# A hybrid decoder trunk on one core: the mixer's weights are split in two pieces of 512 columns instead of four of 256

## The chip, the core and the metric

The kernel runs on one core of a Trainium2 chip (trn2). The metric is the device time of one execution in microseconds. Before the change the median of three runs is 1102.03 us, from 1096.82 to 1108.56. About 1% (11 us) is what a measurement of this kernel can tell from no change.

## What is computed

Two layers (DEPTH = 2) over 256 tokens of 1024 channels, all in float32:

```python
for l in range(DEPTH):
    x = layer_norm(ALPHA * x + swiglu_half(x, ffn1_w1[l], ffn1_w3[l], ffn1_w2[l]), ln1_g[l], ln1_b[l])
    h = x @ w_in[l]
    (a_u, a_v, b_qkv, b_z, b_beta, b_decay, c_q, c_k, c_v, c_r, c_g) = jnp.split(h, split_at, axis=-1)
    out_a = spatial_gating(...)     # chunked gating MLP
    out_b = gated_deltanet(...)     # short conv, triangular solve in chunks of 64, scan over 4 chunks
    out_c = gla(...)                # gated linear attention, chunks of 64
    x = layer_norm(ALPHA * x + concat([out_a, out_b, out_c]) @ w_out[l], ln2_g[l], ln2_b[l])
    x = layer_norm(ALPHA * x + swiglu_half(x, ffn2_w1[l], ffn2_w3[l], ffn2_w2[l]), ln3_g[l], ln3_b[l])
```

## The kernel before

All weights stand in one array `w_all` of units, each 128 partitions by 1024 float32 columns (eight 128x128 tiles). A layer has 167 units: 66 of the first FFN, 35 of the mixer, 66 of the second FFN. A unit is loaded by one DMA into a raw buffer (five of them, SP's queue), then turned into two tiles of the type fp32r: `wh` is the rounded weight (a cast on ACT, L199), `wl` is what the rounding left out (raw minus `wh`, a subtraction on DVE, L200). The activations are split likewise into xH and xL, and one float32 product is three matmuls (`mm3`, L227 to L229: wh·xH, wh·xL, wl·xH). There are five `wh` and five `wl` buffers. `done` (L212) converts ahead, so that two units lie converted behind the one just finished.

`conv` (L184) cuts a unit's conversion into pieces: one cast and one subtraction each. The number of pieces comes from `CUTS` (L41) by the unit's place i in the mixer: one piece for i < 9 (the seven units misc, m, z, r and the first two k units), four pieces for i from 9 to 34, one in the FFNs. Four mixer units of each layer (`WHOLE`, L55: au0, cv0, cv1, v3) are multiplied raw, with no conversion. So 26 - 4 = 22 units of a layer, 44 in all, are converted in four pieces of 256 columns. A loop over pieces issues cast, subtraction, cast, subtraction; a new load of the raw buffer is asked for after the last piece (L202).

Each engine takes its instructions in one fixed order. The order is made at build time by a scheduler, which places what is ready and goes by priorities and its own costs. `ORDER` (L42) is the order in which the mixer's tasks are handed to it, `PIN` (L43) names tasks that may not come ahead of the end of the solve.

The mixer of a layer runs like this. The units misc, m, z, r; then four k and four q units with a short convolution behind each (L565, three times L567); the squares of q and k are summed on PE (`pss`, L698), ACT takes logarithms (L724), and DVE builds the decay matrices (L726 to L782). `t_sub` (L817 to L836) is a long chain on DVE that inverts 16x16 blocks; its end is L834, called the solve here. PE has filler meanwhile: pcv, pau, pav, pv, and transposes of k (`ptk`, L895). Then `t_l0` and `t_l1` join the blocks with small matmuls (p1a L850, L852 on DVE, p2a L856, p1b L870, p2b L877), with v and z units as filler. Then the scan over four chunks: `t_s` (pX), `t_d` and `t_dk` (the matrix XP, L924, L932; POOL's product qd at L933), `t_c` (S at L1075, u, po), and the output projection `yo`. The unit pau1 needs the PSUM bank that L932 frees.

Of the kernel before, what the change touches and what calls it, by code (L numbers as in the profile page):

```python
# [37 lines left out]
HP0, HP1, HP2, HP7 = 0, 400, 300, 0  # L38
CONST = 3
EVAC = 12  # L40
CUTS = ((9, 1), (17, 4), (35, 4))  # L41
ORDER = "v0 sub cv a0 tk0 zz av v3 v1 l0a l0b z3 l1a v2 zr l1b tk1 avn tv z1 zm s0 cq s1 d1 d0 dk a1 c0 pp kt t0 sc s2 c1 t1 s3 c2 pz w1 po c3 t2 w3 t3 w0 w2".split()  # L42
PIN = set("tk0 av v3 v1 l0a z3 l1b tk1 avn z1 s1 pp t0 s2 c1 c2 w1 po c3 t3 w2".split())  # L43
UNITS = {"a0": ("au", 0), "a1": ("au", 1), "av": ("av", 0), "cv": ("cv", 0), "v0": ("v", 0), "v1": ("v", 1),
# [79 lines left out]
def trunk(ctx: ExitStack, tc: tile.TileContext, xin, w_all, cin, pin, lin, gin, out, dbg=None, nlayers=L):  # L124
# [59 lines left out]
    def conv(upto):  # L184
# [11 lines left out]
        i = b % NU - 3 * NF  # L196
        w = 1024 // next((c for o, c in CUTS if 0 <= i < o), 1)
        for o in range(0, 1024, w):
# [1103 lines left out]
```

## Time and profile before

| what | value |
|---|---|
| median of the runs | 1102.03 us |
| the profiled execution | 1108.28 us, of which the span from first to last instruction is 1106.5 us |
| busy: PE, DVE, ACT, POOL | 1062.1, 753.9, 600.4, 78.6 us |
[...]
| conversions on DVE (L200) and ACT (L199) | 413.8 and 353.2 us, 455 instructions each |

A busy PE is not a PE at full speed: matmuls overlap in the pipeline, and a matmul that was issued while the clock stood at half speed takes about twice as long. In the FFN stretches PE issues a matmul of 256 columns every 0.11 us. The mixers lie at about 189 to 345 us and 736 to 897 us of the span.

### The profile page before, as it was taken

The page shows a single profiled execution, that of the slowest core. Times are in us where ns is not written, and L with a number is a line of the kernel's source. Part 1 is how long each engine was busy: PE and PEld are TensorE (multiplying, and loading weights), DVE is VectorE, ACT ScalarE, POOL GpSimd, SP SyncE. Part 2 cuts the span into 40 slices and gives each one's busy share as a digit, 9 for nine tenths or more (in the row PEclk, how much of TensorE's full clock was granted, in tenths as well). Part 3 has the DMA queues.
Part 4 walks back from the last instruction along what each step waited for, and adds up shares of the span by engine and source line. Part 5 has one row for each costly group of instructions (what it writes and reads, how often), then busy time and mean ns, then how long its engine had stood idle before and what let it go on. Part 6 is the DMA issues. An engine that isn't in the chain of part 4 may idle for free. (4 is left out here: it accounts for less than half of the span.)

```text
span 1106.5 us, 23698 instructions
## 1 busy us (share of the span) xinstructions
PE 1062.1 (96%) x9875; PEld 1012.5 (92%) x9875; DVE 753.9 (68%) x1262; ACT 600.4 (54%) x1063; POOL 78.6 (7%) x62
## 2 busy tenths in 40 slices
PE   8999999999999899999989999999989998999996
PEld 7999999987889899999889999999787897999995
DVE  4555556989867965555786555579896679655556
ACT  5444445777556744444664444468664567444442
POOL 0100001101002200000220000020000012000000
PEclk9999999999999999999989999999996999999999
DMA  8855554442323375555336656534331234655541
GB/s 275 303 194 193 193 198 161 153 135 77 116 78 123 138 244 191 192 195 198 140 118 225 193 195 198 195 136 162 124 114 62 97 115 154 229 195 191 191 165 39
DMA packets 51515, 182.38 MB, mean 165 GB/s; under 512 B 5840, under 2 KB 7376, under 8 KB 51280
## 3 DMA queue, kind: packets, MB, share of 16 engines
q1 hardware_dynamic: 50544, 177.23, 47.6%
q10 hardware_dynamic: 864, 3.64, 0.9%
q8 instruction: 77, 1.26, 0.4%
q14 instruction: 30, 0.25, 0.1%
HBM read 179.81 MB, written 1.05 MB: 163 GB/s over the span
## 5 line engine op out<-in xcount | busy, mean ns | idle before, releaser
L200 DVE TENSOR_TENSOR wl<-raw,wh 128x1024 fp32r<-128x1024 f32 (+1 forms) x455 | 413.8, 926 | 236.9 <-ACT wh L199 236.6
L199 ACT CAST wh<-raw 128x1024 fp32r<-128x1024 f32 (+1 forms) x455 | 353.2, 800 | 365.8 <-issue 183.1
L227 PE MATMUL h<-x,wh 128*128 128x256 f32 x864 | 238.7, 276 | 0.0
L228 PE MATMUL h<-x,wh 128*128 128x256 f32 x864 | 238.6, 276 | 0.0
L229 PE MATMUL h<-x,wl 128*128 128x256 f32 x864 | 238.6, 276 | 0.0
L228 PEld LDWEIGHTS h<-x,wh 128*128 128x128 f32 x864 | 162.2, 188 | 0.8
L227 PEld LDWEIGHTS h<-x,wh 128*128 128x128 f32 x864 | 162.2, 188 | 0.7
L229 PEld LDWEIGHTS h<-x,wl 128*128 128x128 f32 x864 | 162.2, 188 | 0.0
L227 PE MATMUL y<-gs,wh 128*128 128x256 f32 x528 | 147.0, 279 | 7.2 <-ACT gs L232 7.2
L228 PE MATMUL y<-gs,wh 128*128 128x256 f32 x528 | 147.2, 279 | 0.0
L229 PE MATMUL y<-gs,wl 128*128 128x256 f32 x528 | 147.1, 279 | 0.0
L228 PE MATMUL h<-xL,wh 128*128 128x256 f32 (+1 forms) x472 | 132.9, 282 | 2.3 <-DVE xL L342 2.1
L227 PE MATMUL h<-xH,wh 128*128 128x256 f32 (+1 forms) x472 | 134.0, 284 | 0.8 <-ACT wh L199 0.7
L229 PE MATMUL h<-xH,wl 128*128 128x256 f32 (+1 forms) x472 | 133.2, 282 | 0.5 <-DVE wl L200 0.5
L227 PEld LDWEIGHTS y<-gs,wh 128*128 128x128 f32 x528 | 100.1, 190 | 7.6 <-ACT gs L232 7.6
L228 PEld LDWEIGHTS y<-gs,wh 128*128 128x128 f32 x528 | 100.6, 191 | 0.0
L229 PEld LDWEIGHTS y<-gs,wl 128*128 128x128 f32 x528 | 100.5, 190 | 0.0
L228 PEld LDWEIGHTS h<-xL,wh 128*128 128x128 f32 x472 | 90.5, 192 | 3.2 <-DVE xL L342 2.9
L227 PEld LDWEIGHTS h<-xH,wh 128*128 128x128 f32 x472 | 90.6, 192 | 1.7 <-ACT wh L199 1.2
L229 PEld LDWEIGHTS h<-xH,wl 128*128 128x128 f32 x472 | 90.5, 192 | 1.0 <-DVE wl L200 0.9
L430 DVE TENSOR_TENSOR g<-s,h 128x256 f32<-128x256 f32 x76 | 32.0, 421 | 45.8 <-PE h L229 37.3
L345 POOL TENSOR_TENSOR s<-x 128x512 f32<-128x512 f32 x5 | 7.1, 1416 | 520.7 <-DVE x L338 520.7
(363 smaller groups left out, 1960.9 us busy)
## 6 DMA issues: line engine op xcount, KB each, us to landing
raw<-w_all SPq DMA_DIRECT2D x331, 512.0 KB, 3.7
raw<-w_all SPq DMA_DIRECT2D x12, 128.0 KB, 4.1
pl<-pin ACTq DMA_DIRECT2D x2, 730.5 KB, 7.2
cst<-cin ACTq DMA_DIRECT2D x1, 1026.0 KB, 8.6
x<-xin SPq DMA_DIRECT2D x4, 256.0 KB, 4.2
out<-xT SPq DMA_DIRECT2D x4, 256.0 KB, 2.0
Gb<-gin ACTq DMA_DIRECT2D x1, 512.0 KB, 3.5
Bb<-gin ACTq DMA_DIRECT2D x1, 512.0 KB, 4.0
```

Of the source, the lines that this page charges most:

```text
L199: st["copy"] = A.copy(WH[b][:, o:o + w], raw[b][:, o:o + w])
L200: V.tensor_sub(WL[b][:, o:o + w], raw[b][:, o:o + w], WH[b][:, o:o + w].bitcast(F32))
L227: PE.matmul(o, lhsT=wh, rhs=mh, start=first, stop=False, **kw)
L228: PE.matmul(o, lhsT=wh, rhs=ml, start=False, stop=False, **kw)
L229: PE.matmul(o, lhsT=wl, rhs=mh, start=False, stop=last, **kw)
L345: G.tensor_tensor(s2, x[:, 0:2], xs, op=ALU.add)
L430: V.tensor_mul(g, s, h3[:, :T])
```

## The change

```diff
-CUTS = ((9, 1), (17, 4), (35, 4))
+CUTS = ((9, 1), (35, 2))
```

`conv` reads the table: the 44 units are cut in two pieces of 512 columns instead of four of 256. ACT has 88 casts fewer and DVE 88 subtractions fewer; the columns converted, the loads and the matmuls are the same. The orders of POOL and SP are the same, word for word; PE has the same matmuls in a slightly different order. The scheduler moved other work too, in both layers alike; three places follow, those of layer 0.

PE at the end of the k and q units, where `pss` is the last of the four sums of squares (pcv is a unit multiplied raw, pv a v unit). Before:

```order
L227 MATMUL pv_3075<-xH,wh_2882 128x256
L228 MATMUL pv_3075<-xL,wh_2882 128x256
L229 MATMUL pv_3075<-xH,wl_2883 128x256
L631 MATMUL pcv<-raw_2715,x 128x256 x2
L698 MATMUL pss<-sqkq,cst 32x512
L631 MATMUL pcv<-raw_2715,x 128x256 x2
L631 MATMUL pcv<-raw_2758,x 128x256 x4
```

After:

```order
L227 MATMUL pv_3043<-xH,wh_2858 128x256
L228 MATMUL pv_3043<-xL,wh_2858 128x256
L229 MATMUL pv_3043<-xH,wl_2859 128x256
L631 MATMUL pcv<-raw_2703,x 128x256
L698 MATMUL pss<-sqkq,cst 32x512
L631 MATMUL pcv<-raw_2703,x 128x256 x3
L631 MATMUL pcv<-raw_2742,x 128x256 x2
```

The last `pss` stands behind one matmul of pcv instead of two. Further on, 16 transposes `ptk` stand ahead of p1a instead of 27 (the 11 others come right behind it), and 8 matmuls of the z unit ahead of p2a instead of 13. On DVE, one of four L586 (for the z and m units) moved from behind L726 to ahead of it; between L726 and the solve no piece stands before or after.

DVE right behind the solve (kb, kd: scaled transposes; wl: the pieces; acc: the convolution of a v unit; iv at L852: what p2a waits for). Before:

```order
L904 TENSOR_TENSOR kb<-ptk,es 128x512
L905 TENSOR_TENSOR kd<-ptk,kds 128x512
L200 TENSOR_TENSOR wl_3272<-raw_2930,wh_3271 128x256 x4
L200 TENSOR_TENSOR wl_3284<-raw_2932,wh_3283 128x256 x4
L567 SCALAR_TENSOR_TENSOR acc<-pv_3295,pl,acc 128x255
L200 TENSOR_TENSOR wl_3337<-raw_2944,wh_3336 128x256
L567 SCALAR_TENSOR_TENSOR acc<-pv_3295,pl,acc 128x254
L200 TENSOR_TENSOR wl_3337<-raw_2944,wh_3336 128x256
L567 SCALAR_TENSOR_TENSOR acc<-pv_3295,pl,acc 128x253
L200 TENSOR_TENSOR wl_3337<-raw_2944,wh_3336 128x256 x2
L567 SCALAR_TENSOR_TENSOR acc<-pv_3311,pl,acc 128x255
L852 TENSOR_TENSOR iv_3062<-p1a,cst 128x256
```

After:

```order
L904 TENSOR_TENSOR kb<-ptk,es 128x512
L905 TENSOR_TENSOR kd<-ptk,kds 128x512
L200 TENSOR_TENSOR wl_3236<-raw_2902,wh_3235 128x512 x2
L200 TENSOR_TENSOR wl_3244<-raw_2904,wh_3243 128x512 x2
L567 SCALAR_TENSOR_TENSOR acc<-pv_3251,pl,acc 128x255
L200 TENSOR_TENSOR wl_3293<-raw_2912,wh_3292 128x512
L567 SCALAR_TENSOR_TENSOR acc<-pv_3251,pl,acc 128x254
L200 TENSOR_TENSOR wl_3293<-raw_2912,wh_3292 128x512
L567 SCALAR_TENSOR_TENSOR acc<-pv_3251,pl,acc 128x253
L567 SCALAR_TENSOR_TENSOR acc<-pv_3267,pl,acc 128x255
L852 TENSOR_TENSOR iv_3030<-p1a,cst 128x256
```

Six pieces instead of twelve stand ahead of the first L852.

DVE ahead of L932 (which frees the bank for pau) and of L1075 (the first state S of the scan). Before:

```order
L971 COPY_PREDICATED PTs<-cst,pPT 128x512 x2
L200 TENSOR_TENSOR wl_4138<-raw_3346,wh_4137 128x256
L932 TENSOR_TENSOR XP<-pkq,XP 128x512
L200 TENSOR_TENSOR wl_4138<-raw_3346,wh_4137 128x256
L932 TENSOR_TENSOR XP<-pkq,XP 128x512
L200 TENSOR_TENSOR wl_4138<-raw_3346,wh_4137 128x256 x2
L200 TENSOR_TENSOR wl_4242<-raw_3529,wh_4241 128x256 x4
L200 TENSOR_TENSOR wl_4290<-raw_3605,wh_4289 128x256
L1075 COPY S<-pS 128x256
```

After:

```order
L971 COPY_PREDICATED PTs<-cst,pPT 128x512 x2
L200 TENSOR_TENSOR wl_4074<-raw_3298,wh_4073 128x512
L200 TENSOR_TENSOR wl_4174<-raw_3477,wh_4173 128x512
L932 TENSOR_TENSOR XP<-pkq,XP 128x512 x2
L200 TENSOR_TENSOR wl_4174<-raw_3477,wh_4173 128x512
L200 TENSOR_TENSOR wl_4218<-raw_3549,wh_4217 128x512
L1075 COPY S<-pS 128x256
```

Two pieces of 512 stand between L971 and the first L932 instead of one of 256, and the piece right ahead of L1075 has 512 columns instead of 256. That piece's cast on ACT, too, is the first instruction behind ACT's wait for pau in both orders.

## Rows read from the trace of the kernel before

**Rows 1.** The page's first part: busy us, share of the span, instructions.

```profile
PE 1062.1 (96%) x9875; PEld 1012.5 (92%) x9875; DVE 753.9 (68%) x1262; ACT 600.4 (54%) x1063; POOL 78.6 (7%) x62
```

**Rows 2.** Windows, mixer of layer 0: stretch, length, busy us (instructions) of PE, PEld, DVE, ACT, POOL, PEclk, DMA.

```profile
211.00:245.00 34.00, 34.00 (x299) 29.41 (x297) 31.41 (x84) 27.21 (x70) 0.00 (x0) 1.00 0.43 144
272.90:299.60 26.70, 24.83 (x554) 22.38 (x554) 21.27 (x56) 12.90 (x32) 0.00 (x0) 0.87 0.32 103
```

**Rows 3.** Windows, mixer of layer 1: the stretch from p1a to pX.

```profile
819.70:852.20 32.50, 30.43 (x552) 27.25 (x552) 21.76 (x58) 13.32 (x32) 0.00 (x0) 0.68 0.26 83
```

**Rows 4.** Waits of PE, 185 to 350 us: us in total, times, longest.

```profile
PE p1a L850 <- DVE iv L833: 1.9, 1, 1.9
PE pau L227 <- DVE XP L932: 1.9, 1, 1.9
PE p2a L856 <- issue: 1.7, 1, 1.7
```

**Rows 5.** Waits of PE, 743 to 908 us.

```profile
PE p1a L850 <- DVE iv L833: 2.8, 1, 2.8
PE p1b L870 <- issue: 2.1, 1, 2.1
```

**Rows 6.** Groups of instructions by form: count, busy us, mean ns, idle before.

```profile
L200 DVE TENSOR_TENSOR wl<-raw,wh 128x256 fp32r<-128x256 f32 x176 | 71.8, 446 | 6.9 <-ACT wh L199 6.8
```

**Rows 7.** Timeline, DVE: start us, us from first start to last end, line, form, count.

```profile
209.84 1.89 DVE L384 TENSOR_TENSOR x<-x,rs 128x512 f32<-128x512 f32 x3
...
274.68 2.75 DVE L200 TENSOR_TENSOR wl<-raw,wh 128x256 fp32r<-128x256 f32 x8
```

**Rows 8.** Timeline, ACT: four casts of 256; a cast of 512 and its follower.

```profile
234.68 1.31 ACT L199 CAST wh<-raw 128x256 fp32r<-128x256 f32 x4
...
331.89 0.61 ACT L232 CAST mAC<-mc 128x512 fp32r<-128x512 f32 x1
332.41 0.47 ACT L166 ACTIVATE sqb<-pqb,cst 128x256 f32<-128x256 f32 x1
```

**Rows 9.** Timeline, PE, around the last pss and the transposes behind it.

```profile
243.21 1.02 PE L631 MATMUL pcv<-raw,x 128*128 128x256 f32 x4
244.16 1.04 PE L698 MATMUL pss<-sqkq,cst 128*32 128x512 f32 x2
...
255.96 1.50 PE L895 MATMUL ptk<-cst,KQ 64*64 64x64 f32 x44
```

**Rows 10.** Timeline, ACT: the squares that the last pss reads.

```profile
242.05 0.64 ACT L703 ACTIVATE sqkq<-KQ 128x512 f32<-128x512 f32 x1
```

**Rows 11.** Timeline, DVE, around L726; in brackets: idle before, and its releaser.

```profile
242.88 0.88 DVE L586 SCALAR_TENSOR_TENSOR zrm<-muN,zrm 128x256 f32<-128x256 f32 x2
...
245.74 0.41 DVE L726 SCALAR_TENSOR_TENSOR RT<-lnn,gam 8x256 f32<-8x256 f32 x1 [1.31 <-ACT lnn L166]
```

**Rows 12.** Timeline, DVE, ahead of the first L852: layer 0, then layer 1.

```profile
279.19 0.75 DVE L200 TENSOR_TENSOR wl<-raw,wh 128x256 fp32r<-128x256 f32 x2
280.08 0.48 DVE L567 SCALAR_TENSOR_TENSOR acc<-pv,pl,acc 128x255 f32<-128x255 f32 x1
...
826.65 0.48 DVE L567 SCALAR_TENSOR_TENSOR acc<-pv,pl,acc 128x255 f32<-128x255 f32 x1
827.04 0.42 DVE L852 TENSOR_TENSOR iv<-p1a,cst 128x256 f32<-128x256 f32 x1
```

**Rows 13.** Timeline, DVE, ahead of the first L932.

```profile
305.73 1.95 DVE L200 TENSOR_TENSOR wl<-raw,wh 128x256 fp32r<-128x256 f32 x1
```

**Rows 14.** Timeline, POOL, at the same time.

```profile
305.05 2.35 POOL L933 TENSOR_TENSOR qd<-qd,KQ 128x1024 f32<-128x1024 f32 x1 [1.09 <-ACT qd L166]
```

**Rows 15.** Timeline, ACT and then DVE, behind the unit pau.

```profile
312.88 0.40 ACT L199 CAST wh<-raw 128x256 fp32r<-128x256 f32 x1 [5.57 <-PE pau L228]
...
313.31 0.42 DVE L200 TENSOR_TENSOR wl<-raw,wh 128x256 fp32r<-128x256 f32 x1 [2.08 <-ACT wh L199]
```

**Rows 16.** Waits of PE, 312.9 to 345 us: all there are.

```profile
PE pu L1058 <- DVE S L1077: 0.2, 1, 0.2
```

## The prediction

> **What bounds the kernel now.** First the page's busy times: PE is busy for 1062.1 us of a span of 1106.5 us, DVE for 753.9, ACT for 600.4 [rows 1]. PE does the bulk of the work, so an edit on ACT and DVE can only win time where PE waits for them, or where PE runs below its full clock because it has waited. Next, the windows of the mixer of layer 0. While the k and q units run (211 to 245 us) PE is busy for all 34.00 us at clock 1.00, although DVE is busy for 31.41 of them [rows 2]: there the conversions are hidden. [...] Last the waits of PE: for the solve 1.9 and 2.8 us, for L932 1.9 us, and 1.7 and 2.1 us in the middle of p2a or p1b for which the profile names nobody [rows 4, 5]. All waits of a mixer come to some 6 or 7 us; that is nearly all that there is to win or lose, apart from the clock.
>
> **What the change takes off ACT and DVE.** 176 pieces of 256 columns [rows 6] become 88 of 512. The mean durations there must not be multiplied, since one piece starts before the last has ended. In a run, eight pieces take 2.75 us, 0.344 each; three subtractions or products of 512 columns take 1.89 us, 0.63 each [rows 7]. A unit on DVE goes from 4 x 0.344 = 1.38 to 2 x 0.63 = 1.26 us, 0.12 less. On ACT four casts take 1.31 us in a run; a cast of 512 takes 0.61 us and lets its follower start 0.52 us after itself [rows 8], so two take 0.52 + 0.61 = 1.13, 0.18 less. Over 44 units that is 5.3 us off DVE and 7.9 us off ACT. Half of it belongs to either layer, and most lies beside a PE that doesn't wait. [...]
>
> **The change place by place**, against the profiled execution (1108.28 us, 6.3 above the median of the runs; a difference found in it is taken off the median as it is). Bounds are for both layers together.
>
> *The k and q units: 0.* The second pair of xL now stands behind two pieces of 512 instead of two of 256, 2 x (0.63 - 0.344) = 0.57 us later, and the first matmuls on it can slip as much. PE now has a third k unit's matmuls to put there. Bounds 0 and +1.1; I take +0.2. That a matmul waits for a whole piece costs nothing while the unit was converted two units ahead, as now; without that cover a unit would wait 0.63 - 0.344 = 0.29 us.
>
> *The solve: -1.0.* The last pss runs at 244.16, though its squares are done at 242.05 + 0.64 = 242.69 [rows 9, 10]: it waits in PE's queue behind two matmuls of pcv, 244.16 - 243.21 = 0.95 us. With one ahead it comes 0.48 us earlier. ACT's logarithms follow, then L726, which now waits 1.31 us [rows 11]; a moved L586 (0.88 / 2 = 0.44 us) fits in that wait and leaves the chain behind it. Together the solve could end 0.48 + 0.44 = 0.92 us earlier in each mixer. But 11 transposes now come behind p1a: 44 rows of them (two rows a transpose) take 1.50 us [rows 9], so 22 rows are 0.75 us that PE has still to do. Where PE sets the pace behind p1a, the gain is 0.17; where the chain does, 0.92. The stretch is mixed [rows 2, 3], so I take the middle, 0.5 a layer. Bounds -1.8 and 0.
>
> *Behind the solve: -0.4.* The first L852 now has six pieces ahead instead of twelve: 6 x 0.63 - 12 x 0.344 = -0.35 us. In layer 0 DVE is done with its pieces at 279.94 and waits until 280.08 for a convolution that PE feeds, so the gain is hidden; in layer 1 it doesn't wait, and L852 follows at once [rows 12]. One layer gains: -0.4 in round numbers; bounds -0.7 and 0.
>
> *Ahead of L932: +0.6.* The piece in front of it took 1.95 us, where another took 0.42 [rows 15], while POOL ran its product for 2.35 us [rows 13, 14], from 305.05 to 307.40: the piece ended 0.28 us behind that. After the change two pieces stand there. If the second falls under the product, it ends later by 0.29 us, what 512 columns cost more than 256; if the first does, the second comes on top, 0.63. PE's pau waits for L932 already [rows 4], so this goes on the path. I take 0.3 a layer; bounds 0 and +1.3.
>
> *Ahead of the first S: +0.6.* ACT stands 5.57 us in a wait for pau, and the first thing behind is a cast; DVE waits 2.08 us for it before its piece, and S comes behind [rows 15]. Cast and piece grow by 0.52 - 0.33 = 0.19 and 0.29 us, 0.48 together. PE's only recorded wait up to the end of the mixer is 0.2 us for an S [rows 16], so some of this is hidden by other small matmuls. I take 0.3 a layer; bounds 0 and +1.0.
>
> Sum: 0.2 - 1.0 - 0.4 + 0.6 + 0.6 = 0.0, between -2.5 and +3.4. From the profiled 1108.3 that stays 1108.3, and from the median 1102.0. POOL and SP keep their orders, so that no load or product is asked for at another place; the FFNs are as they were.
>
> **The rivals.** *The clock comes back.* What ended 5.8 us later in layer 1 than in layer 0 is the same work at a lower clock [rows 2, 3]. Each of these stretches begins behind a wait of PE for the solve [rows 4, 5]. The change moves these waits and the work around them; if layer 1 then runs like layer 0, the time is 1102 - 5.8 = 1096. All of both low-clock parts would give 0.13 x 26.7 + 0.32 x 32.5 = 13.9 us, 1088. For it: it differs already between two layers. Against it: the solve still comes after PE's filler, since p1a's wait stays at 1.9 - 0.92 + 0.75 = 1.7 us.
>
> *The clock goes lower: the other side.* Only 8 matmuls of z stand ahead of p2a, not 13; at 34.00 / 299 = 0.114 us a matmul [rows 2], 5 x 0.114 = 0.6 us of filler is gone where PE needs L852's result. A new wait there would follow that for the solve closely. If layer 0 then runs as layer 1 does, the time is 1102 + 5.8 = 1108; if both lose as much, 1114. It decides as soon as L852 ends behind z's eighth matmul. [...]
>
> *Coarse pieces stall PE.* If the conversions were only just in time, each of the 44 units would wait 0.29 us: 12.8 us, 1115. Against it: 34.00 busy of 34.00 us in the k and q stage [rows 2].
>
> *ACT is worth more than the rows say.* If ACT's queue held up the chain at every unit and saved the 0.18 us of rows 8 and DVE the 0.12 of rows 7 one behind the other, 44 x 0.30 = 13.2 us would go: 1089. Against it: ACT is busy for 12.90 of 26.70 us behind the solve [rows 2]. [...]
>
> **How the numbers follow.** Terms cancel: 0.53. Clock comes back in one layer: 0.17, in both: 0.04. Clock lower in one layer: 0.15, in both: 0.04. Coarse pieces: 0.04. ACT worth more: 0.03. The likeliest is 1102.0 us, alone between 1099.5 and 1105.4 by the bounds. The range takes in one layer's clock either way and the runs' own spread (1096.82 to 1108.56): 1094 to 1110. Both-layer cases and the last two, 0.15, lie outside. Faster by over 1% (under 1091): 0.07; slower by over 1% (over 1113): 0.08; within 1%: 0.85. About 1% is what a measurement of this kernel can tell from no change.
>
> **What would show it.** The groups of instructions should have 88 pieces of 512 columns at some 0.69 us on DVE and 0.61 on ACT; if these are much longer, the sum is wrong. The solve should end 0.9 us earlier counted from the first k matmul, with p1a's wait between 1.5 and 2 us. L852 of layer 1 should come 0.4 us sooner behind kb; PE's wait for L932 should be as long or 0.3 us longer. PE should still not wait in the k and q stage. The windows behind the solve should have mean clocks between 0.68 and 0.87; a clock outside that in both layers would make the prediction wrong, as would a wait of several us of PE for `wh` or `wl`.

## The result, and the profile after

| | before | changed |
|---|---|---|
| median of 20 runs each, us | 1102.42 (1095.63 to 1112.93) | 1095.03 (1088.96 to 1103.85) |
| ratio changed / before, 95% interval | | 0.9935 [0.9905, 0.9964] |
| profiled execution, us (span) | 1108.28 (1106.5) | 1099.81 (1097.9) |

All ratios, and the mean clocks given with them, leave out executions that took over 1.5% longer than the fastest of the same kernel.

The changed kernel is faster by 0.65%, some 7 us. That is within the 1% that was called no change, and inside the range of 1094 to 1110; but the forecast was that the terms cancel, at 1102, and they don't.

First the page's busy times and the groups by form of the changed kernel (columns as in [rows 1] and [rows 6]):

```profile
PE 1057.2 (96%) x9875; PEld 1009.1 (92%) x9875; DVE 744.0 (68%) x1174; ACT 593.2 (54%) x975; POOL 80.0 (7%) x62
```

```profile
L200 DVE TENSOR_TENSOR wl<-raw,wh 128x512 fp32r<-128x512 f32 x88 | 58.6, 689 | 6.7 <-ACT wh L199 6.2
L199 ACT CAST wh<-raw 128x512 fp32r<-128x512 f32 x88 | 51.7, 616 | 21.6 <-PE pz L228 7.1 <-PE pau L228 4.9 <-PE pr L228 2.9
```

The pieces cost what was forecast (0.69 and 0.61 us). DVE and ACT are busy for 10 and 7 us less; that as such is worth nothing, as the experiments show. Now waits of PE in the mixer of layer 0, then of layer 1 (us in total, times, longest), to be held against [rows 4] and [rows 5]:

```profile
PE p1a L850 <- DVE iv L833: 2.3, 1, 2.3
PE pz L229 <- issue: 2.1, 1, 2.1
PE pau L308 <- ACT cv L642: 0.9, 1, 0.9
```

```profile
PE p1a L850 <- DVE iv L833: 2.4, 1, 2.4
PE pmisc L228 <- DVE xL L342: 1.0, 1, 1.0
PE pau L308 <- ACT cv L642: 0.9, 1, 0.9
PE pv L229 <- DVE wl L200: 0.6, 1, 0.6
```

One more of the trace before belongs beside them, in layer 1:

```profile
PE pau L227 <- DVE XP L932: 1.8, 1, 1.8
```

Two things are gone: in both layers PE's wait for L932 (1.9 us in [rows 4], 1.8 in layer 1), and in layer 1 the wait at p1b that the profile gives to "issue", that is, to nobody (2.1 us [rows 5]). In layer 0 such a wait stays (1.7 before, 2.1 now). The windows from p1a to pX, layer 0 and layer 1 of the changed kernel, against the second row of [rows 2] and against [rows 3]:

```profile
278.90:304.40 25.50, 23.36 (x574) 21.18 (x574) 21.51 (x46) 12.20 (x24) 0.00 (x0) 0.93 0.37 121
820.90:845.90 25.00, 24.41 (x574) 22.37 (x574) 21.61 (x46) 12.21 (x24) 0.00 (x0) 0.86 0.37 116
```

Layer 0 goes from 26.70 to 25.50 us, layer 1 from 32.50 to 25.00, at a mean clock of 0.86 in place of 0.68. Where the clock of layer 1 came from shows in a finer cut. Before, PE at work until 831.1, the wait, and what follows:

```profile
825.00:831.10 6.10, 6.09 (x180) 5.51 (x180) 5.95 (x17) 2.89 (x9) 0.00 (x0) 1.00 0.69 214
831.10:833.10 2.00, 0.00 (x0) 0.00 (x0) 1.26 (x4) 0.21 (x1) 0.00 (x0) 1.00 0.00 0
833.10:838.00 4.90, 4.85 (x63) 4.35 (x63) 1.86 (x5) 1.66 (x5) 0.00 (x0) 0.67 0.50 166
834.80:851.90 17.10, 17.10 (x195) 15.14 (x195) 8.20 (x22) 6.52 (x14) 0.00 (x0) 0.50 0.13 44
```

The same work in the changed kernel:

```profile
830.80:834.40 3.60, 3.60 (x163) 3.40 (x164) 3.55 (x9) 0.72 (x2) 0.00 (x0) 1.00 0.04 15
834.40:838.00 3.60, 3.60 (x76) 3.22 (x70) 2.64 (x6) 1.96 (x5) 0.00 (x0) 1.00 0.52 166
838.00:842.00 4.00, 4.00 (x81) 3.47 (x81) 3.80 (x11) 1.99 (x4) 0.00 (x0) 1.00 0.37 121
```

Before, PE ran no instruction at all for 2.0 us, and then ran at half its clock (0.50) for 17.1 us although it was busy all the time; matmuls of 256 columns started 0.215 us apart there (834.58 to 836.30 us, records of 0.41 us each) and 0.115 at 1.00 (829.50 to 830.42 us, records of 0.28). In the changed kernel there is no such gap and the clock stays at 1.00. From the first p2a to the first pX that is 24.3 us before and 15.1 after (827.9 to 852.2, 830.8 to 845.9): the wait of 2.1 us, and 7 us that go with the low clock. The wait for the solve, at the start of these stretches, is in both kernels, and in both the clock is low behind it, in the changed kernel for longer. Layer 1, before and then changed:

```profile
821.10:824.50 3.40, 3.38 (x23) 3.11 (x22) 3.40 (x10) 1.86 (x6) 0.00 (x0) 0.51 0.17 39
```

```profile
822.70:829.50 6.80, 6.21 (x44) 5.88 (x43) 5.26 (x12) 2.22 (x6) 0.00 (x0) 0.50 0.59 181
```

Behind pX, up to the first po, layer 0 goes from 14.2 to 11.2 us, layer 1 from 14.1 to 11.2. The two windows of layer 0, before and after:

```profile
299.60:313.80 14.20, 12.35 (x179) 10.33 (x178) 12.12 (x26) 8.55 (x18) 4.65 (x3) 0.88 0.37 124
```

```profile
304.40:315.60 11.20, 11.20 (x193) 9.28 (x192) 8.59 (x17) 8.69 (x16) 4.89 (x3) 1.00 0.46 153
```

These differences come to 14.6 us (1.2 + 7.5 + 3.0 + 2.9), twice the gain of the medians. The profiled execution of before lies 6 us above its median, and that of the changed kernel lost 7 us in the first FFN, which the change doesn't touch (last section): the trace shows where time went, the medians how much.

### The profile page after: what moved, and what is told of

Same layout as the page of the kernel before. It is cut to its first block, busy times and chain, and to the rows that moved or that the text cites. A ratio compares the mean times of both kernels' runs of the same rounds, so it can differ in the third digit from the quotient of the medians.

```text
span 1097.9 us, 23518 instructions
## 1 busy us (share of the span) xinstructions
PE 1057.2 (96%) x9875; PEld 1009.1 (92%) x9875; DVE 744.0 (68%) x1174; ACT 593.2 (54%) x975; POOL 80.0 (7%) x62
## 3 DMA queue, kind: packets, MB, share of 16 engines
q8 instruction: 77, 1.26, 0.5%
## 4 chain that ended last, share of the span: by engine, by line
PE 77%; DVE 17%; issue 3%; ACT 2%; DMA 1%; DVEq 0%; SPq 0%; ACTq 0%
PE h L229 13%; PE h L228 13%; PE h L227 13%; PE y L227 5%; PE y L228 5%; PE y L229 5%; DVE wl L200 4%; PE y L520 2%; PE y L522 2%; PE y L521 2%; DVE xL L342 2%; PE h L308 1%; DVE acc L567 1%; DVE x L338 1%; PE yo L227 1%
## 5 line engine op out<-in xcount | busy, mean ns | idle before, releaser
L200 DVE TENSOR_TENSOR wl<-raw,wh 128x1024 fp32r<-128x1024 f32 (+1 forms) x367 | 400.0, 1098 | 241.4 <-ACT wh L199 240.5
L199 ACT CAST wh<-raw 128x1024 fp32r<-128x1024 f32 (+1 forms) x367 | 342.8, 946 | 369.1 <-issue 192.1
```

The source lines that it names most:

```text
L199: st["copy"] = A.copy(WH[b][:, o:o + w], raw[b][:, o:o + w])
L200: V.tensor_sub(WL[b][:, o:o + w], raw[b][:, o:o + w], WH[b][:, o:o + w].bitcast(F32))
```

## The experiments

Three explanations of the 7 us stood at first: the place (PE's wait for L932 and what hangs on it), the spread (0.17 us at each of the 44 units), and the front (the solve comes sooner). The first four runs tried these. They turned up a fourth, the instructions, which the other eight runs test; in those, theory P stands for all explanations by the pieces themselves.

All results in one table. "Issue" are PE's waits for nobody, of 0.4 us or more, behind p1a; p2a to pX and pX to po are taken from the first starts of these tiles in the trace, to some 0.1 us; "clock" is the mean granted clock of a kernel's executions (of before beside them: 0.980, 0.982, 0.978 and 0.981 in the four sets of runs: 1 to 4, 5 to 8, 9 to 11, 12).

| kernel | ratio to before, 95% | clock | issue L0 / L1, us | p2a to pX, L0 / L1 | pX to po, L0 / L1 |
|---|---|---|---|---|---|
| before | | | 1.7 / 2.1 | 18.2 / 24.3 | 14.2 / 14.1 |
| changed | 0.9935 [0.9905, 0.9964] | 0.986 | 2.1 / 0 | 17.4 / 15.1 | 11.2 / 11.2 |
| 1: k and q in two | 0.9991 [0.9952, 1.0029] | 0.980 | 1.7 / 1.6 | 16.8 / 23.9 | 14.2 / 10.4 |
| 2: later units in two | 0.9949 [0.9913, 0.9986] | 0.985 | 2.4 / 0 | 17.7 / 15.6 | 11.2 / 11.2 |
| 3: before, pieces held | 0.9986 [0.9945, 1.0028] | 0.978 | 1.6 / 1.7 | 18.2 / 23.9 | 10.3 / 10.3 |
| 4: before, POOL later | 0.9989 [0.9951, 1.0027] | 0.982 | 2.2 / 2.6 | 17.3 / 26.0 | 11.0 / 10.8 |
| 5: before, shift 128 | 0.9964 [0.9928, 1.0000] | 0.983 | 0 / 1.2 and 1.1 | 14.8 / 16.3 | 14.2 / 14.2 |
| 6: before, shift 256 | 1.0008 [0.9966, 1.0049] | 0.983 | 0.8 / 0.8 | 15.9 / 15.8 | 12.7 / 14.2 |
| 7: changed, shift 128 | 0.9904 [0.9865, 0.9944] | 0.985 | 0 / 0 | 15.1 / 15.1 | 11.2 / 11.2 |
| 8: changed, shift 40 | 0.9912 [0.9875, 0.9948] | 0.985 | 0 / 0 | 15.0 / 15.8 | 11.1 / 11.2 |
| 9: before, shift 160 | 0.9913 [0.9877, 0.9949] | 0.985 | 0.8 / 0 | 15.9 / 14.9 | 14.2 / 14.2 |
| 10: pieces held, shift 160 | 0.9872 [0.9824, 0.9920] | 0.987 | 0.7 / 0 | 15.8 / 14.9 | 10.1 / 10.1 |
| 11: changed, shift 64 | 0.9885 [0.9841, 0.9929] | 0.986 | 0 / 0.9 | 15.1 / 16.3 | 11.2 / 11.2 |
| 12: changed, shift 256 | 0.9906 [0.9870, 0.9942] | 0.986 | 2.2 / 0.4 | 17.6 / 15.7 | 11.1 / 11.1 |

### 1 and 2: half of the units each

```
-CUTS = ((9, 1), (17, 4), (35, 4))
+CUTS = ((9, 1), (17, 2), (35, 4))
```

and, for the second,

```
-CUTS = ((9, 1), (17, 4), (35, 4))
+CUTS = ((9, 1), (17, 4), (35, 2))
```

> Only the k and q units and v0 (7 units a layer, 14 in all) are cut in two; all later units stay in four. The change as a whole won 7 us (1102.4 to 1095.0). Theory A, the place: the gain is PE's wait for L932 (1.9 us in layer 0, 1.8 in layer 1) and the low clock behind it, pX to the first po going from 14.2 to 11.2 us; here the pieces ahead of L932 are as before, so PE's wait for L932 stays near 1.9 us and the time within 2 us of before. Theory B, the gain is spread over the 44 units, 7.4 / 44 = 0.17 us each: 14 x 0.17 = 2.4 us faster. Theory C, the front: the solve comes sooner (my own term, -1.0) and brings clock with it: 3 to 6 us faster, p1a to pX shorter in layer 1 than before's 24 to 32 us.

> Only the units behind v0 (15 units a layer, 30 in all) are cut in two; k, q and v0 stay in four. Theory A, the place (PE's wait for L932): no piece stands between L954 and L971 any more, the wait is gone, 6 to 7 us faster than before, as the whole change. Theory B, spread: 30 x 0.17 = 5.1 us faster. Theory C, the front: 0 to 3 us faster.

Measured: 0.9991 and 0.9949. The later units carry the gain; the k and q units, and with them the front, have none that can be told. The gain of the second, 0.51% or 5.6 us, lies between what A and B said, so the time does not part these two. The trace does more: in 1 the wait at p1b is there (1.6 us, layer 1 from p2a to pX 23.9 us), in 2 it is gone (15.6 us), as in the changed kernel. In 2, too, eight matmuls of z stand ahead of p2a, and in 1 thirteen.

### 3: the pieces of w3 and w0 held behind L932

```
-            V.tensor_sub(WL[b][:, o:o + w], raw[b][:, o:o + w], WH[b][:, o:o + w].bitcast(F32))
+            r = V.tensor_sub(WL[b][:, o:o + w], raw[b][:, o:o + w], WH[b][:, o:o + w].bitcast(F32)); 28 <= i < 30 and behind(r, st["dk"])
...
-                V.tensor_tensor(PT[:, cs], pkq[c2], XP[:, cs], op=ALU.mult)
+                st["dk"] = V.tensor_tensor(PT[:, cs], pkq[c2], XP[:, cs], op=ALU.mult)
```

> The kernel before, all pieces still 256 columns; only the pieces of w3 and w0 are held behind the second L932, so that none stands between L954 and L932 (before: seven, one of which took 1.95 us). Theory A, the place: L932 runs 2 to 3 us sooner, PE's pau does not wait for it, 4 to 7 us faster (3.7 us of waits in both layers, more if the clock behind it stays up). Theories B and C: within 1 us of before, since no unit and nothing ahead of the solve is changed.

Measured: 0.9986 [0.9945, 1.0028]. The place is mended as meant. DVE's timeline around L932, in which L932 now waits for PE and not PE for it:

```profile
303.27 1.59 DVE L971 COPY_PREDICATED PTs<-cst,pPT 128x512 f32<-128x512 uint32 x2
305.52 0.69 DVE L932 TENSOR_TENSOR XP<-pkq,XP 128x512 f32<-128x512 f32 x1 [0.66 <-PE pkq L745]
306.38 0.69 DVE L932 TENSOR_TENSOR XP<-pkq,XP 128x512 f32<-128x512 f32 x1 [0.17 <-PE pkq L745]
306.99 3.44 DVE L200 TENSOR_TENSOR wl<-raw,wh 128x256 fp32r<-128x256 f32 x9
```

From pX to po takes 10.3 us and not 14.2. Yet the gain is 1.5 us where 4 to 7 were expected; by the interval it could be up to 6 us. So theory A is not shown to be the cause of the 7 us, nor is it out for a part of them (runs 9 and 10). What this kernel has still in common with before is the two issue waits (1.6 and 1.7) and the long stretch from p2a to pX in layer 1 (23.9 us). The expectation counts seven pieces between L954 and L932; in the trace of before there are four ahead of the first L932 and a fifth ahead of the second.

### 4: POOL's product behind L932

```
-            G.tensor_tensor(qd, qd, KQ[:, :, 1], op=ALU.mult)
+            first = G.tensor_copy(mx.tile([P, 4], F32, tag="after", name="after"), PT[:, 2:4, 0:2, 63]); behind(G.tensor_tensor(qd, qd, KQ[:, :, 1], op=ALU.mult), first)
```

> The kernel before, all pieces 256 columns and in their old places; only POOL's product L933 is made to wait until the second L932 is done (a copy of 4 columns from its result stands ahead of it on POOL). If the piece ahead of L932 took 1.95 us because POOL's product ran beside it: that piece takes about 0.42 us, L932 comes some 1.5 us sooner, PE's wait for it falls from 1.9 to about 0.4 us, 2 to 4 us faster, unless PE then waits for qd at the po of S (a wait of PE there would show it). If the piece is slow for another reason: it stays near 2 us, the wait stays, and the time is within 1 us of before.

Measured: 0.9989. The trace is of an execution of 1110.47 us, long for this kernel. The same instructions as in [rows 13] and [rows 14], DVE first, then POOL:

```profile
311.39 0.41 DVE L200 TENSOR_TENSOR wl<-raw,wh 128x256 fp32r<-128x256 f32 x1
311.72 0.68 DVE L932 TENSOR_TENSOR XP<-pkq,XP 128x512 f32<-128x512 f32 x1
```

```profile
313.68 2.56 POOL L933 TENSOR_TENSOR qd<-qd,KQ 128x1024 f32<-128x1024 f32 x1
```

The piece takes 0.41 us where it took 1.95 [rows 13], now that POOL's product runs behind it (from 313.68 us): the product beside it drew it out. In before, the piece started under the product and ended 0.28 us behind it [rows 13, 14]. L932, with one input in PSUM, takes 0.69 us under the product in the changed kernel (its lines are in the section on the forecast) and 0.68 without it here. PE's wait for L932 in layer 0 is down to 0.3 us:

```profile
PE pau L227 <- DVE XP L932: 0.3, 1, 0.3
```

In time it is again too little to be told. The two issue waits are there (2.2 and 2.6 us).

### What the traces showed then

PE's issue waits stand at the same place of PE's stream in before, in the changed kernel and in runs 1 to 4. PE runs one LDWEIGHTS and one MATMUL for each of the 9875 rows, 19,750 instructions; the page of the changed kernel counts the packets of the instruction queue (77 in before too):

```profile
q8 instruction: 77, 1.26, 0.5%
```

1.26 MB in 77 packets is 16 KB each, and 19,750 / 77 is some 256 instructions each. Counted so, the wait of layer 0 is ahead of number 5042 (5044 in the changed kernel and in run 1), and that of layer 1, where there is one, ahead of 15256 (15258 in runs 1 and 3). With PE's own instructions for semaphores counted too, 5057 or 5058 stand ahead of the one and 15297 or 15298 ahead of the other, in all six traces. From the one to the other before has 10,214 of the former and 26 for semaphores: 10,240, just 40 blocks of 256. So PE waits where a block starts. PE's timeline at the two places of before, then of the changed kernel:

```profile
281.35 1.28 PE L856 MATMUL p2a<-iv 32*32 32x32 f32 x125
284.29 0.25 PE L856 MATMUL p2a<-iv 32*32 32x32 f32 x3 [1.66 <-issue]
...
830.63 0.47 PE L870 MATMUL p1b<-iv,AT 32*32 32x32 f32 x17
833.15 0.44 PE L870 MATMUL p1b<-iv,AT 32*32 32x32 f32 x15 [2.05 <-issue]
```

```profile
286.98 1.31 PE L856 MATMUL p2a<-iv 32*32 32x32 f32 x128
...
290.92 0.38 PE L229 MATMUL pz<-xH,wl 128*128 128x256 f32 x1 [2.08 <-issue]
...
834.11 0.69 PE L870 MATMUL p1b<-iv,AT 32*32 32x32 f32 x32
```

p2a is 128 rows, 256 instructions, in 1.3 us: a whole block. In layer 0 of before the block from 4786 to 5042 is nearly all p2a. In layer 1 the one from 15000 starts at 828.14, inside p2a, and is done at 831.1, 3.0 us later. The queues of the DMA engines in these stretches of before, 828 to 830.5 us and 830.5 to 832 us (packets, MB, share of 16 engines):

```profile
q1 hardware_dynamic: 138, 0.49, 60.2%
```

```profile
q8 instruction: 1, 0.02, 3.9%
q1 hardware_dynamic: 4, 0.00, 0.8%
```

The next packet starts when the weights' loads have ended, at 830.74, 2.6 us after the block, and PE goes on at 833.15, 2.4 us after the packet's start. In the other seven such waits of 1.6 us or more, in before, in the changed kernel and in runs 1 to 3, PE went on 2.2 to 2.5 us after such a packet's start. In the changed kernel PE's order has p2a five matmuls, ten instructions, earlier, and seventeen matmuls of z instead of twelve between p2a and p1b. The block from 15000 starts at 831.1, its packet 0.8 us later, and its last instruction is reached at 834.4, 3.3 us after its first: no wait. In before the last instruction was reached at 830.9, 2.8 us after the first. So the other order gave 0.5 us, the sooner packet 1.8: by these two traces most of the wait of 2.1 us went with the packet, and not with the order.

### 5 and 6: the stream moved by half a block, and by a whole one

```
-    one.tile([P, 32], F32, name="pad")
+    zz = one.tile([P, 32], F32, name="pad")
...
-    for t in (RT, gam, Qbd, PTs):
+    for t in (zz, RT, gam, Qbd, PTs):
         G.memset(t, 0.0)
...
+    pad = ybank(0, "pad"); [PE.matmul(pad[:32, :32], lhsT=zz, rhs=zz, start=True, stop=True) for _ in range(32)]
     for k in range(KD):
         split(xN[0][:, k], xN[1][:, k], x[:, k])
```

Run 6 has 64 in place of 32.

> The kernel before, with 32 matmuls of 32x32 on zeros ahead of the first FFN (into a bank that is overwritten later); each is 4 instructions on PE, so all that follows stands 128 instructions further on in PE's stream and is otherwise as before. Theory I, PE runs dry of instructions: the two waits in the middle of p2a and p1b for which the profile names nobody always stand at the same instruction (number 5042 in layer 0, 15256 or 15258 in layer 1, counted in the traces of four kernels), a multiple of 256 apart from where a 16 KB packet on the instruction queue starts; a block of 256 is run through in under 3 us there (p2a alone is 256) and the next has not landed. Moved by half a block, the boundary falls into the middle of p2a, both waits (1.7 and 2.1 us) go, and with them the low clock behind: p2a to pX 24 to 15 us in layer 1; 8 to 12 us faster than before, 1091 to 1095. Theory P, the pieces: nothing at the solve depends on where an instruction stands in the stream; both waits stay, the time is within 2 us of before.

> The kernel before with 64 such matmuls, 256 instructions, a whole block: the control. Theory I: the boundaries fall on the same matmuls as before, the waits in p2a (1.7 us) and p1b (2.1 us) stay and the time is within 2 us of before. If the added matmuls as such did something, it differs as the shift by 128 does.

Measured: 0.9964 [0.9928, 1.0000] and 1.0008 [0.9966, 1.0049]. The waits of the first, all in layer 1, and those of the second, one in each layer:

```profile
PE p2a L856 <- issue: 1.2, 1, 1.2
PE pv L228 <- issue: 1.1, 1, 1.1
```

```profile
PE p2a L856 <- issue: 0.8, 1, 0.8
PE p1b L870 <- issue: 0.8, 1, 0.8
```

With the whole block the waits are on the same matmuls as before, and the time is that of before: the added matmuls as such do nothing that can be told. With half a block the wait of layer 0 is gone and those of layer 1 stand elsewhere, at two other block starts. So the waits go with the place in the stream. The gain, 4 us, at the edge of its interval, is half of the least that was expected; layer 1 got two new waits, one of them where a block was nearly all p1a. That the same waits took 0.8 us in one execution and 1.7 and 2.1 in another was not expected; it goes with the start of the packet, 1.4 us after its block in the one and 2.6 in the other (layer 1). So run 6 is a control by its times and not by its trace: that execution had short waits and no long stretch of low clock (p1a to pX 24.2 and 25.0 us), and took 1102.07 us with its first FFN at the slower of the two speeds of the last section.

### 7 and 8: the same with the changed kernel

As above, with 32 and 10 added matmuls.

> The changed kernel with the 32 matmuls. Theory I: its one wait of 2.1 us (in layer 0, behind p2a, at instruction 5042 too) goes, layer 1 stays without one; 2 to 5 us faster than the changed kernel (1095.0), and only 2 to 4 us, PE's wait for L932, faster than the kernel before with the same shift. Theory P: as the changed kernel, 1095, and 7 us below the kernel before with the same shift.

> The changed kernel with 10 such matmuls, 40 instructions. In layer 1 the boundary that fell 50 instructions into p2a falls about 10 into it, so that the block is nearly all p2a (some 1.9 us); in layer 0 it moves from the start of p2a to 36 instructions (some 2 us of filler) ahead of it. Theory I: the wait comes back in layer 1, 1.3 to 3 us, with low clock behind it (p2a to pX of layer 1 from 15 to 20 us or more), and in layer 0 it falls to under 1 us; the time lies between 1093 and 1102. Theory P: the waits and p2a to pX stay as in the changed kernel, 1095.

Measured: 1090.47 and 1090.85 us, 0.9904 and 0.9912. Neither shows an issue wait, and both layers go from p2a to pX in 15 to 16 us. For the shift by 40 a wait of 1.3 to 3 us was to come back in layer 1. What is there is 0.6 us ahead of p1b, which the profile gives to PE's own pz; a block starts at that place, 2.3 us after its packet's start, so it can be the same wait, much shorter. Its packet came 1.4 us after the block, which starts some 28 instructions into p2a. The place alone does not decide; the packet's start counts too.

### 9 and 10: without larger pieces

Run 9 is the kernel before with 40 added matmuls; run 10 is that with the edit of run 3.

> The kernel before with 40 of the added matmuls, 160 instructions. The shift by 128 took the waits in layer 0 away but left two of 1.2 and 1.1 us in layer 1, since a block there was nearly all p1a. By 160 a block starts 92 instructions into p2a in layer 0 and 154 into it in layer 1, and p1a has 18 more of filler in its block. Theory I (PE runs dry where a block of 256 instructions is run through too soon): waits for nobody of 1 us or less in all in either layer, p2a to pX 15 to 16.5 us in both, 1094 to 1097. Theory P (pieces): as before, 1102.

> All pieces of 256 columns, as before; the pieces of w3 and w0 held behind the second L932 (as in the earlier experiment) and the stream shifted by 160 instructions: PE's wait for L932 and its waits for instructions are both taken away, without a piece made larger. Theory I: 3 to 5 us faster than the shift alone, 1089 to 1093, that is, as fast as the changed kernel with its own shift (1090.5 and 1090.9): then the size of the pieces as such is worth nothing, and the change's gain was where it left the instructions. Theory P: the saved time of ACT and DVE (0.30 us a unit by the rows) is missing, and the time stays 3 us or more above 1090.9, at 1094 or more.

Measured: 1095.14 us (0.9913 [0.9877, 0.9949]) and 1088.98 us (0.9872 [0.9824, 0.9920]); as theory I said. The windows from p1a to pX of run 9, layer 0 and layer 1:

```profile
272.30:296.70 24.40, 23.39 (x554) 21.10 (x554) 21.18 (x56) 12.89 (x32) 0.00 (x0) 0.93 0.37 114
816.10:839.20 23.10, 23.07 (x553) 20.84 (x553) 21.06 (x56) 12.87 (x32) 0.00 (x0) 0.93 0.38 117
```

This is the decision. With every piece at 256 columns and the same order on all engines (but for two casts of ACT in the first 25 us), 40 idle matmuls at the start of the program take layer 1 from 32.50 us [rows 3] to 23.10, and the ratio lies clear of that of the control, run 6. With L932's wait removed too, the kernel with four pieces is at 1089, no slower than any with two. Cutting weights in two pieces is worth nothing as such that these runs could tell; run 10 also has the lowest median of all. L932's wait, 3.7 us in the trace, fits the difference of runs 9 and 10: 0.9872 / 0.9913, 0.4%, though their intervals overlap.

### 11 and 12: the wait put back, and the control

The changed kernel with 16 and with 64 added matmuls.

> The changed kernel with 16 of the added matmuls, 64 instructions: it puts the wait back where the change took it away. In layer 1 a block starts 4 instructions into p2a and ends with it, as it does in layer 0 of the changed kernel, where that cost 2.1 us; in layer 0 it starts 58 instructions ahead of p2a. Theory I: a wait for nobody of 1.5 to 2.5 us in layer 1 at the end of p2a, none in layer 0; p2a to pX of layer 1 17 to 24 us in place of 15.1, that of layer 0 15 in place of 17.4; 1094 to 1100 in all, 3 to 9 us slower than the changed kernel shifted by 40 (1090.9). Theory P: 1091 to 1095 with both layers as in the changed kernel.

> The changed kernel with 64 of the added matmuls, a whole block of 256 instructions: the control to the changed kernel's shifts by 128, 40 and 64, which all came to 1090.5 to 1090.9. Theory I (where a block of instructions starts): the blocks start on the same matmuls as in the changed kernel, so its wait at the end of p2a in layer 0 (2.1 us) is back and layer 1 has none; p2a to pX of layer 0 16 to 17.5 us; 1093 to 1097, ratio to the kernel before 0.992 to 0.995. If the added matmuls themselves did it, 1090 to 1091 again, ratio 0.988 to 0.991, and no wait in layer 0.

Measured: 1090.88 (0.9885) and 1091.48 us (0.9906 [0.9870, 0.9942]). PE's waits in layer 1 of the first, then in layer 0 of the second:

```profile
PE pz L227 <- issue: 0.9, 1, 0.9
```

```profile
PE pz L228 <- issue: 2.2, 1, 2.2
```

In run 11 the wait is where it was said to come, at the end of p2a, but half as long, and the time is as without it; this attempt to undo the gain failed. In run 12 the wait of layer 0 is back on its matmul (17.6 us from p2a to pX), as theory I said, and yet the time is 1091.5 and the ratio 0.9906, which is what was expected if the added matmuls themselves did it. In the kernel before they did not (run 6); for the changed kernel this stays open. So the wait that the changed kernel keeps in layer 0 costs too little to be told by these runs, and the gain of 4 us that runs 7 and 8 seemed to show over the changed kernel may be none.

### The clock of all executions

A trace shows one execution; the mean granted clock is on record for each. In the kernel before it falls into two groups: of the 89 executions behind the ratios, 43 have 0.970 to 0.980, with a median of 1106.0 us, and 46 have 0.982 to 0.988, with 1098.6. The long stretch at 0.50, 17.1 of 1106 us, takes 0.008 from a mean, about what parts the two; the profiled execution, which has it, has 0.973, and that of run 6, which has not, 0.985. Of runs 1, 3, 4 and 6, whose blocks start on the same matmuls, 21 of 41 executions lie at 0.980 or below; of runs 2 and 7 to 12 none of 69, of run 5 two of 12, of the changed kernel one of 20.

So the kernel before has the slow layer 1 in about half of its executions, and the other half is as fast as the changed kernel but for some 4 us. As an estimate, 43 / 89 x 7.4 = 3.6 us of the median's gain is the end of that stretch, and L932's wait (3.7 us in the trace) can be the rest. Run 3 had 8 of 10 executions in the lower group, which hides a part of what it gained at L932.

## Why the range held and the mechanism was wrong

The likeliest, 1102.0, missed by 7 us. The range held because it took in one layer's clock either way and the spread of the runs; with a mechanism that was not the one at work, that is luck. Two steps failed: the term ahead of L932 had the wrong sign (+0.6, measured -3.7 us), and the waits "for which the profile names nobody" got no term, though one of them, in layer 1, had the long stretch of low clock behind it. Term by term:

*The pieces.* 689 and 616 ns, as forecast, and worth nothing beside a PE that does not wait for them. The rivals "coarse pieces stall PE" and "ACT is worth more" are out: one wait of 0.6 us for a piece in all of layer 1, and run 10.

*The k and q units, +0.2, and the solve, -1.0.* From the first k matmul to p1a it is 61.6 and 61.1 us before, 60.4 and 60.7 after: 1.6 sooner for both layers, where 0.8 was taken and 1.8 was the bound. p1a's wait, 2.3 and 2.4 us, is longer than the 1.5 to 2 that were forecast. All the same run 1, which has the changed k and q units, has no gain that can be told.

*Behind the solve, -0.4.* Wrong in this trace: in layer 1 L852 came 7.97 us behind kb (821.49 to 829.46) and not 6.74 as before; it waited for a convolution that PE fed late, at a mean clock of 0.61 from 825 to 830.8 us. Run 12, the same order of instructions, has 7.9 us from p1a to p2a in layer 1 where this trace has 9.9 and before had 8.2.

*Ahead of L932, +0.6.* Wrong in sign: -3.7 us, the two waits of PE. The step that failed is "if the second falls under the product": neither did. In the changed kernel both pieces of w3 stand ahead of L954; L971 follows L924 at once, and the two pieces behind it are done before POOL's product has got far. DVE around L932, and POOL:

```profile
307.83 1.58 DVE L971 COPY_PREDICATED PTs<-cst,pPT 128x512 f32<-128x512 uint32 x2
309.31 1.27 DVE L200 TENSOR_TENSOR wl<-raw,wh 128x512 fp32r<-128x512 f32 x2
310.93 0.69 DVE L932 TENSOR_TENSOR XP<-pkq,XP 128x512 f32<-128x512 f32 x1 [0.34 <-PE pkq L745]
```

```profile
310.11 2.70 POOL L933 TENSOR_TENSOR qd<-qd,KQ 128x1024 f32<-128x1024 f32 x1 [1.05 <-ACT qd L166]
```

The forecast kept the place of the pieces relative to POOL's product and only made them longer. It had also to ask what stands between L954 and the first L932 in all, four pieces before and two after.

*Ahead of the first S, +0.6.* From the first po to the start of the last yo it is 39.5 and 38.9 us before, 39.5 and 39.1 after: 0.2, inside the bounds of 0 and 1.0.

*The clock.* The likeliest case said that it stays. The rival "the clock comes back in one layer", 0.17 for 1096 us (5.8 us less, 32.50 of [rows 3] against 26.70 of [rows 2]), is what happened in size (1095.0) and in place (layer 1, 32.50 to 25.00 us). Its cause was wrong. It tied the low clock to PE's wait for the solve; that wait is still there (2.4 us in layer 1, 2.8 before), with 6.8 us of low clock behind it where before had 3.4, while the clock of layer 1 as a whole is back at 0.86. What went is the stretch of 17.1 us behind the issue wait. By the forecast's own sign, a mean clock outside 0.68 to 0.87 in both layers, it was not refuted: layer 0 lay outside, at 0.93, and layer 1 did not. The row that mattered was shown in [rows 5] and set aside: 2.1 us "for which the profile names nobody". The forecast gave the wait itself no term and no case, although it is longer than any other term. The other-side rival watched the same edit, eight matmuls of z ahead of p2a and not thirteen, and priced it as lost filler, +6; by the traces the five that went behind p2a made the block ahead of p1b 0.5 us longer, which is time for the next packet.

What is shown: the issue waits stand at starts of blocks of PE's instructions; the kernel before loses them but for 0.8 us, and 0.9% of its time, when its stream is moved by 160 instructions; four pieces are as fast as two once PE's waits are equal. What is read from traces but not tried alone: why the changed kernel lost its wait in layer 1; the five matmuls account for 0.5 us, the packet that came sooner (0.8 us after the block's start, not 2.6) for more. Why a packet comes late, with the weights' loads or for another reason, was not tried either.

## What to carry to other kernels

A wait that the profile gives to nobody deserves a cause before an edit is priced: count PE's instructions up to it, those for semaphores too, and if it stands at the same number in several kernels, a multiple of 256 from another (here 10,240), it may well be, as here, that PE waits for its instructions, and an edit that moves bursts of small matmuls in PE's stream can win or lose it: here 1.7 and 2.1 us, of which run 9 kept 0.8. Before crediting an edit with a gain of 1%, shift the stream of the kernel before by part of a block: here that alone, with no other edit, was worth as much as the change. A product of 2.35 us on POOL stretched a subtraction beside it on DVE here from 0.41 us (run 4) to 1.95 [rows 13, 14], so look at what stands beside POOL's spans ahead of a result that PE waits for.

## What the runs showed of the hardware that was not expected

- The instruction queue moved 1.26 MB in 77 packets of 16 KB, one for some 256 of PE's 19,750 instructions. Around p2a a packet starts some 0.2 to 4.3 us after PE has begun the block ahead of it (2.6 and 0.8 in layer 1 of before and of the changed kernel), and where PE waits it goes on some 2.2 to 2.7 us after that start (2.4 at the three waits of these two kernels); p2a alone, 256 instructions, is run in 1.3 us. The waits were 0.4 to 2.6 us.
- Behind such a wait PE ran at a granted clock of 0.50 for 17.1 us while it was busy without a gap (834.8 to 851.9 us of before), and in other executions with waits of 0.8 to 1.2 us it did not (15.8 to 16.3 us from p2a to pX). No rule is drawn from that here.
- The first FFN has two speeds at a granted clock of 1.00, before anything that the change touches. From 20 to 180 us, before and changed:

```profile
20.00:180.00 160.00, 160.00 (x1414) 160.00 (x1414) 91.20 (x103) 76.97 (x104) 3.75 (x4) 1.00 0.64 216
```

```profile
20.00:180.00 160.00, 160.00 (x1361) 160.00 (x1360) 87.85 (x100) 73.72 (x100) 4.72 (x4) 1.00 0.62 209
```

  1414 matmuls or 1361 in the same time, with no wait in either; the mixer of layer 0 begins at 188.6 or at 196.0 us. Run 12, with the instructions of the changed kernel, has 1414; run 6, with those of the kernel before, has 1361. So it does not belong to either kernel, and its cause stays open. It can make a part of the difference between the changed kernel and run 12: time times mean clock falls into two groups, and 11 of 20 executions of the changed kernel are in the higher one (1080.5 to 1085.3 us), but 3 of 12 of run 12 (1080.7 to 1082.0). It is one more reason why a single trace says where time goes and not how much.
